# Copies of the key pages: 24 on GpSimd's queue in the index stage, 40 on SyncE's in the retention

## The chip, the cores and the metric

The kernel runs on one core of a Trainium2 chip. The metric is the time of one execution on the device, in microseconds. The kernel before took 1080.78 us, the median of three runs (1079.39 to 1082.35).

A core has engines that work side by side, each through its own list of instructions: PE (TensorE, matrix products; PEld is its loading of weights), DVE (VectorE), ACT (ScalarE), POOL (GpSimd) and SP (SyncE, which here does nothing but start DMA transfers). Sixteen DMA engines move the data that SP, ACT and POOL ask for. SBUF is the core's memory, in 128 partitions; PSUM holds the results of PE.

## The reference

One step of a decoder layer with sparse attention and retention side by side, for a new sequence of 1024 tokens ("prompt") and for 8 x 4 new tokens ("sample") that have 1024 earlier tokens each in a paged cache.

```python
def hybrid_layer(x, c, pos, attn_fn, ret_fn, w_ada, b_ada, g_norm, w_in, g_ret, w_pa, w_pr, w_out):
    B, T, _ = x.shape
    h, gate = modulated_input(x, c, w_ada, b_ada, g_norm)
    qa, ka, va, za, qi, ki, wi, qr, kr, vr, zr, ga, gr = split_projection(h @ w_in)
    heads = lambda a, n: a.reshape(B, T, n, -1)
    ka, va = heads(ka, N_HEADS_A), heads(va, N_HEADS_A)
    y_a = attn_fn(heads(qa, N_HEADS_A), ka, va, heads(qi, N_HEADS_IDX), ki, wi) * jax.nn.silu(za)
    q_r = rotary(heads(qr, N_HEADS_R), pos)
    k_r = rotary(heads(kr, N_HEADS_R), pos) * DK_R ** -0.5
    ret, ret_state = ret_fn(q_r, k_r, heads(vr, N_HEADS_R).astype(jnp.float32))
    y_r = group_norm_heads(ret).astype(x.dtype) * g_ret * jax.nn.silu(zr)
    merged = jax.nn.sigmoid(ga) * (y_a @ w_pa) + jax.nn.sigmoid(gr) * (y_r @ w_pr)
    x = x + gate[:, None, :] * (merged @ w_out)
    return x, (ka, va, ki, ret_state)

def dsa_sample(q, k_new, v_new, qi, ki_new, wi, cache_k, cache_v, cache_kidx, page_table):
    ...
    ki_past = cache_kidx[page_table].reshape(DB, PAST_LEN, HEAD_DIM_IDX)
    ki_all = jnp.concatenate([ki_past.astype(ki_new.dtype), ki_new], axis=1)
    idx, valid = select_keys(index_scores(qi, wi, ki_all), pos, topk)
    ...
    kg = jnp.where(in_past[..., None, None], cache_k[phys, slot].astype(k_new.dtype), take_rows(k_new, idx_n))
    ...
    return sparse_attend(q, kg, vg, valid).reshape(DB, T, WIDTH_A)
```

D_MODEL is 1024, there are 8 heads of 64 in attention and retention and 4 of 64 in the indexer, and everything is float32. What matters here is `cache_k`: the kernel computes the logits of the sample tokens against all 1024 past keys of each of the 8 sequences, so it needs all 8 x 8 = 64 pages that the page table names. A page is 128 tokens x 8 heads x 64, 256 KB.

## The kernel before

**Projections.** `h @ w_in` is made 128 columns at a time. Each such projection (`project_parts`, L532 to L550) runs over three pieces of 352 of the 1056 tokens and, in each, over 8 slices of the contraction with three products (`terms`, L224 to L228), since weights and activations are split into a high and a low part. SP loads 128 columns of weights, 512 KB, into `ws` (`wload`, L205); ACT takes the high part (L211), and DVE, or POOL for each third projection, the low part (`wsplit`, L212). `prefetch` (L513 to L524) is called at the head of each projection. It starts loads of later projections in the order of the list `order` (L505 to L510): the index queries, four gates (O_GA), then for each pair of retention heads K, Q, V, Z of the retention (O_KR, O_QR, O_VR, O_ZR), the attention's queries (O_QA) and two gates, and after the four pairs the attention's keys, values and the rest. Loads run about two projections ahead of their use.

**Stages.** In the profiled execution the index stage lies at about 74 to 133 us and the retention at 133 to 545 us. The index stage scores the prompt's queries in blocks b = 7 to 2, with four heads h each (L903 to L927); then it gathers the indexer's cached keys with eight indirect DMAs of POOL into `kx` (L963), two buffers in turn, and PE transposes them (L969). The retention (L620) handles two heads at a time in `pair` (L673). K and Q are rotated there: SP loads the table `rot` (L692), and once the projection is done it copies halves of the rows crosswise into `tmp` (L696 and L697, the swaps); then three full-size operations make the rotated rows (L699 to L701). These run on POOL for both rows of pair 0 and pair 1 and for K of pair 2, and on DVE for the others (`e = nc.vector if p + a > 2 else nc.gpsimd`). PE then makes state products (L735), DVE scans them (L737), ACT copies the result to `SD` (L739); PE makes the scores (L747), DVE multiplies them with the decay masks (L753), and PE forms the outputs (L763, L766). Further work of a pair is on POOL: `qm` (L781), `vm` (L785), and the two full-size steps of the group norm (L813 and L821), the last of which PE waits for in order to transpose (L829). Beside all this DVE and ACT pick the 256 best keys of each token by counting passes (L996 to L1091, with short steps such as L1022, L1062 and L1089).

**The page copies.** `KG` (L576) is a buffer in DRAM that holds each sequence's past keys with the head halves apart; SP reads it back as `kv` (L1221), from 558 us on, when the retention is over. `copy_page` (L580 to L592) fills it, one page a call. It is one call ahead of itself: ACT copies the page table's column for the next page to a small tile `ptn` (L585); for the page of the call before, POOL reads the number of the page from its tile (L589) and starts a DMA from `cache_k` to `KG`, DRAM to DRAM, 256 KB (L590). There are 12 calls in the index scoring, at every second head (L923), then one in nine of sixteen pieces of every projection (`turn`, L546 and L547), and at the end, after the first key projection of the attention, whatever is left (L1290 and L1291). In the trace the 64 issues lie between 74.5 and 541.1 us.

**Order.** Each engine executes its instructions in one fixed order. A scheduler makes it from the program as it is written and from when operands should be ready, and may move an instruction ahead of others that are written earlier; `tc.issue_after(x)` is a constraint that the instructions under it stand behind x in that order.

Of the kernel before, what the change touches and what calls it, by code (L numbers as in the profile page):

```python
# [34 lines left out]
O_QA, O_KA, O_VA, O_ZA, O_QI, O_KI, O_QR, O_KR, O_VR, O_ZR, O_GA, O_GR = (  # L35
    0, 512, 1024, 1536, 2048, 2304, 2372, 2884, 3396, 3908, 4420, 5444)
# [88 lines left out]
def _hybrid_step(ctx, tc, A, outs, dbg):  # L125
    nc = tc.nc
# [17 lines left out]
    def pj():  # L144

        turns[0] += 1
        if third[0] and turns[0] % 3 == 0:
            return third[0].tile([128, 512], F32, name="pj3", bufs=1)
        return psj.tile([128, 512], F32, name="pj", bufs=2)

    def pl():
        return ps.tile([128, 1024], F32, name="pl", bufs=2)

    def pt():
        return ps.tile([128, 512], F32, name="pt", bufs=2)
# [47 lines left out]
    def wload(pool, src, f0, n, k=KT, name="ws", bufs=2):  # L203
        ws = pool.tile([128, k, 128], F32, name=name, bufs=bufs)
        nc.sync.dma_start(ws[:, :, :n], wcols(src, k, f0, n))  # L205
        return ws

    def wsplit(pool, ws, n, k=KT):
        wh = pool.tile([128, k, 128], F32R, name="wh", bufs=2)
        wl = pool.tile([128, k, 128], F32R, name="wl", bufs=2)  # L210
        nc.scalar.copy(wh[:, :, :n], ws[:, :, :n])  # L211
        (nc.vector if k == 4 or len(order) % 3 else nc.gpsimd).tensor_sub(wl[:, :, :n], ws[:, :, :n], f32(wh[:, :, :n]))  # L212
        return wh, wl
# [10 lines left out]
    def terms(p, w, k, sl):  # L224
        wh, wl = w
        nc.tensor.matmul(p, wh[:, k], HH[k][:, sl], start=(k == 0), stop=False)  # L226
        nc.tensor.matmul(p, wh[:, k], HL[k][:, sl], start=False, stop=False)  # L227
        nc.tensor.matmul(p, wl[:, k], HH[k][:, sl], start=False, stop=(k == KT - 1))  # L228
# [16 lines left out]
    def last_on(engine):  # L245
        return next(i for i in reversed(nc.cur_bb.bb.instructions) if i.engine == engine)
# [4 lines left out]
    with ExitStack() as s0:  # L251
# [121 lines left out]
        rows_, turn = {}, [0]  # L373
# [56 lines left out]
        v, t, u = [RB[:, T + 9 * i:T + 9 * i + 9] for i in range(3)]  # L430
# [62 lines left out]
        for k in range(KT):  # L493
            for step in steps[k].split():
# [3 lines left out]
                else:  # L498
                    at, o = int(step[1]), int(step[2])
# [13 lines left out]
    def prefetch():  # L513

        while order and len(fetched) < (2 if room[0] else 1):
            f0 = order.pop(0)
            room[1] += 1
            pool = room[0] if room[0] and room[1] % 3 == 0 else wp
            with tc.issue_after(loads[-1].ins):
                fetched.append((f0, wload(pool, w_in, f0, 128, bufs=2 if pool is wp else 1)))  # L520
        if fetched:
            f0, ws = fetched.pop(0)
            with tc.issue_after(head_ends[0].ins), tc.issue_after(head_ends[1].ins):
                split.append((f0, wsplit(wp, ws, 128)))  # L524
# [7 lines left out]
    def project_parts(f0, use, chunks=chunks):  # L532

        if not split:
            prefetch()
        g0, w = split.pop(0)
        assert g0 == f0
        prefetch()
        for c, sl in enumerate(chunks):
            p = pj()[:, :sl.stop - sl.start]  # L540
            for k in range(KT):
                terms(p, w, k, sl)
            end = last_on(mybir.EngineType.PE)
            use(c, p)
            turn[0] += 1
            if turn[0] * 9 // 16 != (turn[0] - 1) * 9 // 16:  # L546
                copy_page()  # L547
            if marks is not None:
                marks.append([last_on(e) for e in (mybir.EngineType.DVE, mybir.EngineType.Activation)])
            yield end  # L550
# [24 lines left out]
    KG = dram.tile([NB, 4, 4, 256, 128], F32, name="KG")  # L575
    pages = []  # L576

    seen, turn = [], [0]

    def copy_page():  # L580
        if pages:
            at = pages.pop(0)
            t = cst.tile([NB, 1], I32, name="ptn", bufs=2)
            with tc.issue_after(last_on(mybir.EngineType.Activation)):
                nc.scalar.copy(t, pages_of[0][:, at[1]:at[1] + 1])  # L585
            seen.append((at, t))
        if len(seen) > (1 if pages else 0):
            (b, g), t = seen.pop(0)
            v = nc.gpsimd.value_load(t[b:b + 1], min_val=0, max_val=A["cache_k"].shape[1] - 1)  # L589
            nc.gpsimd.dma_start(KG[b, g // 2, :, 128 * (g % 2):128 * (g % 2) + 128],  # L590
                              A["cache_k"][0][bass.ds(v, 1)].rearrange("o t (j h) d -> (o j) t (h d)", j=4))

    pages_of = []

# [3 lines left out]
    def split_rows(pool, f0, p, dst, new, x=None):  # L598

        hl = [pool.tile([128, TT], F32R, name="raw", bufs=rows_kept[0]) for _ in "hl"]  # L600

        def use(c, y):
            sl = slice(c * CH, c * CH + CH)
            nc.scalar.copy(hl[0][:, sl], y)
            if x is not None:
                nc.scalar.copy(x[:, sl], y)
            nc.vector.tensor_sub(hl[1][:, sl], y, f32(hl[0][:, sl]))
            if c == 2:
                for k in range(4):
                    nc.scalar.copy(new[32 * p:32 * p + 32, k], y[32 * k:32 * k + 32, CH - NS:])  # L610
        yield from project_parts(f0, use)
        for places, t in zip(dst, hl):
            for d in places:
                nc.sync.dma_start(d[128 * p:128 * p + 128], f32(t[:, :T]))
# [232 lines left out]
    with ExitStack() as s1:  # L847
# [4 lines left out]
        with ExitStack() as s2:  # L852
# [37 lines left out]
            for g in range(3):  # L890
                p = pt().rearrange("p (t c) -> p t c", c=128)
                for t in range(4 * g, min(4 * g + 4, 9)):
                    n = 128 if t < 8 else NS
# [13 lines left out]
            for b in range(7, 1, -1):  # L907
                W = (b + 1) * 128
                for h in range(4):
                    m = -(-W // 512)  # L910
                    p = pl().rearrange("p (m c) -> p m c", c=512)[:, :m, :W // m]
                    q = QS[h][:, b * 128:b * 128 + 128]
                    for n in range(m):
                        sl = slice(n * W // m, (n + 1) * W // m)
                        nc.tensor.matmul(p[:, n], q, KH[:, sl], start=True, stop=False)
                        nc.tensor.matmul(p[:, n], q, KL[:, sl], start=False, stop=True)
                    rl = ip.tile([128, LK], F32, name="rl", bufs=2)
                    nc.scalar.activation(rl[:, :W].rearrange("p (m c) -> p m c", m=m), p, AF.Relu)
                    if h == 0:
                        nc.vector.tensor_scalar(SC[b], rl[:, :W], wsc[:, b, 0:1], None, op0=OP.mult)  # L920
                    else:
                        scored = nc.vector.scalar_tensor_tensor(SC[b], rl[:, :W], wsc[:, b, h:h + 1], SC[b], op0=OP.mult, op1=OP.add)
                    if h % 2:  # L923
                        copy_page()
                if b == 7:
                    whole_row = scored.ins
                nc.vector.tensor_add(SC[b][:, W - 128:W], SC[b][:, W - 128:W], C[:, C_CAUS:C_CAUS + 128])  # L927
# [23 lines left out]
            for G in (0, 1):  # L951
                p = pt()[:, :128]
                nc.tensor.matmul(p, SX[:NS, 128 * G:128 * G + 128], dw.rearrange("p h t -> p (h t)"), start=True, stop=True)
                t = ip.tile([128, 4, NS], F32, name="wt", bufs=2)
# [4 lines left out]
            for G in (0, 1):  # L959
                KP = []  # L960
                for b in range(4 * G, 4 * G + 4):
# [5 lines left out]
                    p = pt()  # L967
# [162 lines left out]
    def token_rows(tl2, x, p, out_p, out_s, dst):  # L1130
        rows = slice(128 * p, 128 * p + 128)

        def use(t0, m, n, y):
            tk = tl2.tile([128, 4, 128], F32, name="tk", bufs=2)
            nc.scalar.copy(tk[:n, :m], y[:n, :m])
            if n == 128:
                nc.sync.dma_start(out_p[0, 0, 128 * t0:128 * t0 + 512, 2 * p:2 * p + 2].rearrange("(t p) h d -> p t (h d)", p=128), tk)
            else:
                nc.sync.dma_start(out_s[0, :, :, 2 * p:2 * p + 2].rearrange("b i h d -> (b i) (h d)"), tk[:n, 0])
            if dst is not None:  # L1140
                nc.sync.dma_start(dst[128 * t0:128 * t0 + m * n, rows].rearrange("(t p) c -> p t c", p=n), tk[:n, :m])
        to_tokens(x, use)
# [141 lines left out]
    for p in range(4):  # L1284
        x = tl2.tile([128, TT], F32, name="kx", bufs=1)
        for c, _ in enumerate(split_rows(tl, O_KA + 128 * p, p, k_rows, ks, x)):
            if c < 2:
                next(past)
        token_rows(tl2, x, p, k_out, ks_out, None)
        while p == 0 and (pages or seen):  # L1290
            copy_page()  # L1291
        next(past), next(past)
    for p in range(4):
        x = tl.tile([128, TT], F32, name="raw", bufs=rows_kept[0])
# [276 lines left out]
    for n_, j in enumerate(line):  # L1571
        if j not in merged:
            load_merged(j)
        t, u = merged[j]
# [133 lines left out]
```

## Time and profile before

| | us |
|---|---|
| median of three runs | 1080.78 (1079.39 to 1082.35) |
| profiled execution, its own time | 1082.81 |
| its span in the trace | 1081.2 |
| DVE busy | 697.9 |
| ACT busy | 457.1 |
| POOL busy, of it page copies | 271.3, 73.0 |

The span is the time from the first to the last event of the trace; the execution's own time is 1.6 us longer. The mean clock granted to PE was 0.991 of full speed. Rows of the profile name an instruction by engine, line and operation, then output <- input with sizes, and `xN` for a number of them. In a timeline a row begins with its start and duration in us, and ends in brackets with how long the engine sat idle before it and whose work ended that. SPq and POOLq are the queues in which these engines issue DMAs and loads.

### The profile page before, as it was taken

The page shows a single profiled execution, that of the slowest core. Times are in us where ns is not written, and L with a number is a line of the kernel's source. Part 1 is how long each engine was busy: PE and PEld are TensorE (multiplying, and loading weights), DVE is VectorE, ACT ScalarE, POOL GpSimd, SP SyncE. Part 2 cuts the span into 40 slices and gives each one's busy share as a digit, 9 for nine tenths or more (in the row PEclk, how much of TensorE's full clock was granted, in tenths as well). Part 3 has the DMA queues.
Part 4 walks back from the last instruction along what each step waited for, and adds up shares of the span by engine and source line. Part 5 has one row for each costly group of instructions (what it writes and reads, how often), then busy time and mean ns, then how long its engine had stood idle before and what let it go on. Part 6 is the DMA issues. An engine that isn't in the chain of part 4 may idle for free. (4 is left out here: it accounts for less than half of the span.)

```text
span 1081.2 us, 20359 instructions
## 1 busy us (share of the span) xinstructions
PE 1051.9 (97%) x7903; PEld 965.6 (89%) x7903; DVE 697.9 (65%) x1538; ACT 457.1 (42%) x981; POOL 271.3 (25%) x227
## 2 busy tenths in 40 slices
PE   7999999999999999998999999999999999999997
PEld 6899799799989989998899998887999999998776
DVE  6875259668877987799834444211356766597665
ACT  5675355454555555323223322221345665442111
POOL 0015427132722531313210003244023333100000
PEclk9999999899999999998999999999999999999999
DMA  9935665375637644563379879786958520556531
GB/s 305 263 86 154 199 178 151 87 206 149 180 97 228 168 129 145 170 176 86 129 254 310 277 240 312 228 297 230 337 201 270 199 90 31 181 177 241 175 108 59
DMA packets 173620, 202.79 MB, mean 188 GB/s; under 512 B 32068, under 2 KB 140500, under 8 KB 172436
## 3 DMA queue, kind: packets, MB, share of 16 engines
q1 hardware_dynamic: 150352, 164.59, 48.0%
q0 software_dynamic: 22656, 36.05, 11.1%
q8 instruction: 62, 1.02, 0.4%
q10 hardware_dynamic: 516, 0.86, 0.2%
q14 instruction: 34, 0.28, 0.1%
HBM read 156.12 MB, written 57.95 MB: 198 GB/s over the span
## 5 line engine op out<-in xcount | busy, mean ns | idle before, releaser
L226 PE MATMUL pj<-hh,wh 128*128 128x352 f32 (+1 forms) x1168 | 384.5, 329 | 0.0
L228 PE MATMUL pj<-hh,wl 128*128 128x352 f32 (+1 forms) x1168 | 379.1, 325 | 0.2 <-POOL wl L212 0.2
L227 PE MATMUL pj<-hl,wh 128*128 128x352 f32 (+1 forms) x1168 | 379.0, 324 | 0.0
L226 PEld LDWEIGHTS pj<-hh,wh 128*128 128x128 f32 x1168 | 220.7, 189 | 10.6 <-issue 9.1
L228 PEld LDWEIGHTS pj<-hh,wl 128*128 128x128 f32 x1168 | 220.7, 189 | 6.9 <-issue 6.1
L227 PEld LDWEIGHTS pj<-hl,wh 128*128 128x128 f32 x1168 | 221.1, 189 | 3.8 <-issue 3.1
L1008 DVE TENSOR_SCALAR_CACHE_REDUCE eq<-sc,cand 128x896 bf16<-128x896 f32 (+4 forms) x155 | 135.8, 876 | 2.6
L590 POOL DMA_DIRECT2D KG<-in_cache_k x64 | 73.0, 1141 | 222.6 <-issue 134.9
L211 ACT CAST wh<-ws 128x1024 fp32r<-128x1024 f32 (+1 forms) x65 | 61.1, 941 | 128.8 <-PE pj L227 81.4
L212 POOL TENSOR_TENSOR wl<-ws,wh 128x1024 fp32r<-128x1024 f32 x18 | 43.3, 2406 | 191.4 <-ACT wh L211 150.4
L212 DVE TENSOR_TENSOR wl<-ws,wh 128x1024 fp32r<-128x1024 f32 (+1 forms) x47 | 56.0, 1191 | 44.9 <-ACT wh L211 39.7
L1393 POOL TENSOR_SCALAR lg<-lg,st 128x1024 f32<-128x1024 f32 (+7 forms) x64 | 47.2, 754 | 110.1 <-DVE st L1390 100.6
L1227 DVE STREAM_TRANSPOSE kt<-kv 128x1024 f32<-128x1024 f32 x32 | 38.6, 1232 | 43.1 <-DMA kv<-KG 42.8
L1385 ACT ACTIVATE lg<-lg,st 128x1024 f32<-128x1024 f32 (+7 forms) x64 | 49.5, 775 | 28.8 <-DVE st L1379 24.5
L1619 PE MATMUL pj<-woh,MH 128*128 128x512 f32 (+1 forms) x136 | 51.4, 378 | 0.0
L1620 PE MATMUL pj<-wol,MH 128*128 128x512 f32 (+1 forms) x136 | 51.2, 377 | 0.0
L1621 PE MATMUL pj<-woh,ML 128*128 128x512 f32 (+1 forms) x136 | 51.2, 377 | 0.0
L1197 POOL DMA_INDIRECT kv<-in_cache_v,idx x32 | 31.6, 988 | 58.8 <-PE sx L1261 41.2
L1015 ACT ACTIVATE ra<-sc,cand 128x1024 bf16<-128x1024 f32 x31 | 35.6, 1147 | 13.5 <-DVE cand L1091 13.4
L1636 ACT ACTIVATE u<-xo 128x512 f32<-128x512 f32 (+2 forms) x19 | 11.6, 609 | 66.4 <-DVE xo L1635 44.0
L839 ACT ACTIVATE raw<-pj 128x352 f32<-128x352 f32 x48 | 22.1, 461 | 35.4 <-PE pj L228 28.9
L1015 ACT ACTIVATE ra<-scs,cand 32x1056 bf16<-32x1056 f32 x31 | 36.4, 1175 | 0.8
(363 smaller groups left out, 1898.8 us busy)
## 6 DMA issues: line engine op xcount, KB each, us to landing
ws<-in_w_in SPq DMA_DIRECT2D x49, 512.0 KB
KG<-in_cache_k POOLq DMA_DIRECT2D x64, 256.0 KB
kv<-KG SPq DMA_DIRECT2D x32, 512.0 KB
rot<-in_rot SPq DMA_DIRECT2D x8, 1056.0 KB
x<-in_w_ada SPq DMA_DIRECT2D x16, 512.0 KB
TG<-raw SPq DMA_DIRECT2D x15, 528.0 KB
wst<-in_w_out SPq DMA_DIRECT2D x12, 512.0 KB
u<-TG SPq DMA_DIRECT2D x8, 528.0 KB
```

The source lines that it names most:

```text
L211: nc.scalar.copy(wh[:, :, :n], ws[:, :, :n])
L212: (nc.vector if k == 4 or len(order) % 3 else nc.gpsimd).tensor_sub(wl[:, :, :n], ws[:, :, :n], f32(wh[:, :, :n]))
L226: nc.tensor.matmul(p, wh[:, k], HH[k][:, sl], start=(k == 0), stop=False)
L227: nc.tensor.matmul(p, wh[:, k], HL[k][:, sl], start=False, stop=False)
L228: nc.tensor.matmul(p, wl[:, k], HH[k][:, sl], start=False, stop=(k == KT - 1))
L590: nc.gpsimd.dma_start(KG[b, g // 2, :, 128 * (g % 2):128 * (g % 2) + 128], A["cache_k"][0][bass.ds(v, 1)].rearrange("o t (j h) d -> (o j) ...
L1008: nc.vector.tensor_scalar(junk[:n, :W], sc, thr[:n, j:j + 1], 0.0, op0=op, op1=OP.add, accum_out=cnt[:n, j:j + 1])
L1015: nc.scalar.activation(junk[:n, :W], sc, AF.Sign, bias=thr[:n, NV + j:NV + j + 1], scale=-1.0, accum_out=cnt[:n, NV + j:NV + j + 1])
L1385: nc.scalar.activation(l, l, AF.Exp, bias=st[:, i, 1:2], scale=-1.0, accum_out=st[:, i, 3:4])
L1619: nc.tensor.matmul(x, MH[:, k, tk], wh[:, k], start=(k == 0), stop=False)
L1620: nc.tensor.matmul(x, MH[:, k, tk], wl[:, k], start=False, stop=False)
L1621: nc.tensor.matmul(x, ML[:, k, tk], wh[:, k], start=False, stop=(k == KT - 1))
```

## The change

24 calls of `copy_page` remain: one for each of the heads 1 to 3 in the index scoring (18), and six in the pieces of the first four gates. At the first projection after that, `copy_page(0)` issues the page that is one behind. The other 40 pages go through `copy_behind`: at the head of the projections of V, Z, the attention's queries and the two gates of each pair, behind the weights load that `prefetch` has just placed, SP reads the numbers of two pages straight from the page table in SBUF (`pts`) and starts the two DMAs. Source, destination and pattern of a transfer are as before (`copy_to`). No `ptn` tile is needed for those 40. The loop that copied what was left is replaced by an assertion that nothing is.

```diff
         prefetch()
+        if f0 < O_KA or O_VR <= f0 < O_GA or f0 >= O_GA + 4 * 128:
+            copy_page(0)
+            copy_behind(2)
         for c, sl in enumerate(chunks):
...
             use(c, p)
-            turn[0] += 1
-            if turn[0] * 9 // 16 != (turn[0] - 1) * 9 // 16:
+            if O_GA <= f0 < O_GA + 4 * 128 and (c + f0 // 128) % 2:
                 copy_page()
...
-    seen, turn = [], [0]
-
-    def copy_page():
-        if pages:
+    seen = []
+
+    def copy_to(e, v, b, g):
+        e.dma_start(KG[b, g // 2, :, 128 * (g % 2):128 * (g % 2) + 128],
+                    A["cache_k"][0][bass.ds(v, 1)].rearrange("o t (j h) d -> (o j) t (h d)", j=4))
+
+    def copy_behind(n):
+        with tc.issue_after(last_on(mybir.EngineType.SP)):
+            for b, g in pages[:n]:
+                copy_to(nc.sync, nc.sync.value_load(pages_of[0][b:b + 1, g:g + 1], min_val=0, max_val=A["cache_k"].shape[1] - 1), b, g)
+        del pages[:n]
+
+    def copy_page(ahead=1):
+        if ahead and pages:
             at = pages.pop(0)
             t = cst.tile([NB, 1], I32, name="ptn", bufs=2)
             with tc.issue_after(last_on(mybir.EngineType.Activation)):
                 nc.scalar.copy(t, pages_of[0][:, at[1]:at[1] + 1])
             seen.append((at, t))
-        if len(seen) > (1 if pages else 0):
+        if len(seen) > ahead:
             (b, g), t = seen.pop(0)
-            v = nc.gpsimd.value_load(t[b:b + 1], min_val=0, max_val=A["cache_k"].shape[1] - 1)
-            nc.gpsimd.dma_start(KG[b, g // 2, :, 128 * (g % 2):128 * (g % 2) + 128],
-                              A["cache_k"][0][bass.ds(v, 1)].rearrange("o t (j h) d -> (o j) t (h d)", j=4))
+            copy_to(nc.gpsimd, nc.gpsimd.value_load(t[b:b + 1], min_val=0, max_val=A["cache_k"].shape[1] - 1), b, g)
...
-                    if h % 2:
+                    if h:
                         copy_page()
...
-        while p == 0 and (pages or seen):
-            copy_page()
+        assert p or not pages and not seen
```

## The prediction

> **What bounds the kernel now.** I read the engine summary of the page first, then one answer of the windows view over the stage in which the copies are issued, then the groups, then the list of PE's waits, and last the timelines of the engines around the waits that belong to this stage.
>
> ```profile
> PE 1051.9 (97%) x7903; PEld 965.6 (89%) x7903; DVE 697.9 (65%) x1538; ACT 457.1 (42%) x981; POOL 271.3 (25%) x227
> ```
> ```profile
> 74.00:133.00 59.00, 58.71 (x371) 52.54 (x370) 28.34 (x49) 26.86 (x57) 30.30 (x26) 1.00 0.57 161
> 133.00:545.00 412.00, 398.79 (x3034) 376.11 (x3027) 333.76 (x725) 189.57 (x385) 142.91 (x94) 0.98 0.54 153
> ```
> ```profile
> L590 POOL DMA_DIRECT2D KG<-in_cache_k x64 | 73.0, 1141 | 222.6 <-issue 134.9
> ```
>
> PE (TensorE) is busy 1051.9 of 1081.2 us, so time is won only where PE now waits or runs at a lower clock. The windows row gives length, busy time of PE, PEld, DVE, ACT and POOL, granted clock, share of DMA and GB/s. In the index stage (74 to 133 us) PE idles 0.3 us; in the retention (133 to 545) it idles 412.00 - 398.79 = 13.2 us, and the clock is 0.98. All 64 copies lie in these two stages. A copy occupies POOL for 1.14 us, because POOL itself issues it: 73.0 us altogether. That is no cost to PE by itself. It costs where DVE or POOL work that PE needs stands behind a copy, and the waits of PE say where that can be:
>
> ```profile
> PE pb L747 <- DVE tmp L753: 5.6, 3, 3.3
> ...
> PE pt L829 <- POOL O L821: 2.1, 1, 2.1
> ...
> PE pt L969 <- DMA kx<-in_cache_kidx,gidx: 0.3, 1, 0.3
> ```
>
> (Sum, count, longest.) PE's scores L747 wait for the masks L753 on DVE, the last transposes L829 for the norm L821 on POOL. Now the timelines of POOL, DVE and PE in pair 0:
>
> ```profile
> 181.79 1.13 POOL L590 DMA_DIRECT2D KG<-in_cache_k  x1
> 182.94 2.46 POOL L701 TENSOR_TENSOR qrT<-qrT,tmp 128x1056 f32<-128x1056 f32 x1
> 185.35 2.41 POOL L212 TENSOR_TENSOR wl<-ws,wh 128x1024 fp32r<-128x1024 f32 x1
> ```
> ```profile
> 182.02 5.77 DVE L1089 TENSOR_TENSOR base<-base,inc 128x7 int32<-128x7 int32 x1
> ...
> 195.10 1.28 DVE L753 TENSOR_TENSOR tmp<-pb,dm 128x512 f32<-128x512 f32 x2
> ```
> ```profile
> 190.46 1.75 PE L747 MATMUL pb<-qrT,krT 64*64 64x128 f32 x40
> ...
> 195.84 1.97 PE L747 MATMUL pb<-qrT,krT 64*64 64x128 f32 x16 [1.19 <-DVE tmp L753]
> ```
> ```profile
> L1089 DVE TENSOR_TENSOR base<-base,inc x31: 155/167/5772, 157.2 to 456.4; 128x7 int32<-128x7 int32 x31
> ```
> ```profile
> 187.80:195.10 7.30, 5.79 (x96) 4.64 (x94) 7.24 (x17) 5.13 (x10) 4.80 (x5) 1.00 0.61 155
> ```
>
> L1089 adds 7 numbers in each partition; its median is 0.167 us (min/median/max in ns), yet this one lasts 5.77 us, from 182.02 to 187.79: it starts while POOL issues a copy and ends when POOL's unbroken string (copy, L701, L212) ends. So a copy between two POOL operations lengthens the time for which DVE is shut out by its own 1.13 us. Behind it DVE is full (7.24 of 7.30) up to the masks at 195.10, for which PE waits 1.19. That is the loss that this change can take away.
>
> **The change part by part.** *Copies leave POOL in the retention.* 24 of 64 stay on POOL (18 in the index scoring, 6 in the first four gates), 40 go to SP. I go through each place where a copy stands in front of work that PE is late for.
>
> ```profile
> 286.05 1.13 POOL L590 DMA_DIRECT2D KG<-in_cache_k  x1
> ```
> ```profile
> L212 DVE TENSOR_TENSOR wl<-ws,wh 128x1024 fp32r<-128x1024 f32 (+1 forms) x47 | 56.0, 1191 | 44.9 <-ACT wh L211 39.7
> ```
> ```profile
> 286.27 4.51 DVE L212 TENSOR_TENSOR wl<-ws,wh 128x1024 fp32r<-128x1024 f32 x1
> ...
> 400.02 0.74 DVE L1022 TENSOR_SCALAR inc<-cnt 128x5 int32<-128x5 f32 x1
> ```
> ```profile
> 307.74 1.83 PE L763 MATMUL pb<-qrT,SD 128*128 128x128 f32 x14 [1.15 <-ACT SD L739]
> ...
> 400.84 1.09 PE L747 MATMUL pb<-qrT,krT 64*64 64x128 f32 x16 [1.10 <-DVE tmp L753]
> ...
> 503.32 1.97 PE L747 MATMUL pb<-qrT,krT 64*64 64x128 f32 x16 [3.35 <-DVE tmp L753]
> ```
> ```profile
> 536.65 0.18 DVE L820 TENSOR_SCALAR rs_y<-rs_y 128x18 f32<-128x18 f32 x1
> ```
> ```profile
> 399.66 1.13 POOL L590 DMA_DIRECT2D KG<-in_cache_k  x1
> ...
> 493.86 1.11 POOL L590 DMA_DIRECT2D KG<-in_cache_k  x1 [0.86 <-ACT kd L713]
> ...
> 537.84 1.14 POOL L590 DMA_DIRECT2D KG<-in_cache_k  x1 [9.61 <-issue]
> 539.00 2.12 POOL L821 TENSOR_TENSOR O<-O,rs_y 128x1152 f32<-128x1152 f32 x1
> ```
> ```profile
> 541.17 1.09 PE L829 MATMUL pt<-C,O 128*128 128x128 f32 x8 [2.11 <-POOL O L821]
> ```
>
> - Pair 0: one copy, 1.13 us, and PE waits 1.19 for what stands behind it: gain 1.13.
> - Pair 1: the same string around 286.05; DVE's L212 takes 4.51 us where its group's mean is 1.191; PE waits 1.15 at 307.74 for SD, made from DVE's scan: gain 1.13.
> - Pair 2: a copy at 399.66 holds L1022 0.74 us where the equally small L1089 has a median of 0.167, at the moment when PE waits 1.10: gain 0.57.
> - Pair 3: a copy of 1.11 heads a string of POOL at 493.86, ahead of the wait of 3.35. Bounds 0 and 1.11; I take the 0.57 of pair 2.
> - End of pair 3: rs_y is there at 536.83, but POOL takes the copy first and L821 starts at 539.00. Without the copy it starts 2.17 earlier; PE waits 2.11: gain 2.11.
>
> Sum 1.13 + 1.13 + 0.57 + 0.57 + 2.11 = 5.5 us. The other removed copies, with their loads and ACT's ptn columns (40 of 64 go), stand where PE does not wait: nothing.
>
> *Index stage.* POOL gets 18 copies where it had 12, 6 x 1.2 = 7 us more, and stands at 30.3 of 59. The cover is that idle half; what it can expose is the gather of kx, which shares POOL's queue:
>
> ```profile
> 94.02 1.18 POOL L590 DMA_DIRECT2D KG<-in_cache_k  x1
> ...
> 97.24 1.53 POOL L963 DMA_INDIRECT kx<-in_cache_kidx,gidx  x1 [2.04 <-PE pt L969]
> ```
>
> Gathers and copies take turns, and PE already waits 0.3 for one kx. Two buffers limit how far gathers run ahead, so a copy more in front of a gather is 1.18 us later for PE. Bounds: 0 (POOL's idle time takes them all) and 4 x 1.18 = 4.7 (one ahead of every second of the eight gathers). I take one, +1.2. The six copies in the gates replace ones that were there; nothing.
>
> *SP.* A copy on SP is a value load and a DMA issue.
>
> ```profile
> L589 POOLq TENSOR_LOAD <-ptn x64: 287/293/1217, 72.8 to 538.7; - x64
> ```
> ```profile
> 465.27 0.39 SPq L205 DMA_DIRECT2D ws<-in_w_in  x1
> ...
> 472.89 0.52 SPq L696 DMA_DIRECT2D tmp<-qrT  x1
> ...
> 474.72 0.77 SPq L697 DMA_DIRECT2D tmp<-qrT  x1
> ```
>
> The load was 0.29 us on POOL, SP's issues here last 0.39 to 0.77, so a copy is about 1 us of SP: 40 us in the 412 of the stage, on a queue that does nothing but issue. That time is covered; uncovered, two copies would put 2 us in front of a swap. What is queued behind a waiting SP instruction are the swaps of the rotation (L696, L697), the state loads and the next weights. The weights run two projections ahead. The swaps do not, and this is what the copies' traffic can reach:
>
> ```profile
> 482.95 1.26 DVE L699 TENSOR_TENSOR qrT<-qrT,rot 128x1056 f32<-128x1056 f32 x1 [0.73 <-DMA tmp<-qrT]
> ```
> ```profile
> 252.00:254.00 2.00, 2.00 (x15) 2.00 (x14) 1.93 (x5) 0.00 (x0) 1.11 (x1) 1.00 0.97 278
> 254.00:258.00 4.00, 4.00 (x27) 4.00 (x26) 2.79 (x11) 3.00 (x6) 0.00 (x0) 1.00 0.24 67
> ```
>
> From 252 to 254 a weights load fills the 16 DMA engines (0.97, 278 GB/s); from 254 to 258 only one copy moves, at a share of 0.24, four engines, 67 GB/s. 256 KB at that rate is 3.8 us, two copies on the same four engines about 7.6. A pair behind the load of 465.27 (1.9 us) leaves those engines some time after 474.5, while the swaps enter from 472.9 to 475.5; DVE already waits 0.73 for them. Bounds for the late swaps: 0 (copies gone in time, or on other engines), and 2.5 in each of pairs 1 to 3. I take 1.5, nearest to pair 3 alone, where DVE has no slack.
>
> Here a rule of the Trainium skill speaks against the change. Its page "DMA: Bandwidth & Descriptors", in the section "Why a DMA increments its semaphore by 16 and not by 1", says that a transfer uses the largest number of engines up to 16 that divides the slowest dimension of both sides (4 here), and that SP's queue always takes the lowest-numbered ones, where GpSimd's takes consecutive engines in turn. The share of 0.24 agrees with four; no run here shows which. By that rule every copy on SP lands on the same four engines as the one before it; by the 0.24 alone they might spread, and the 1.5 would be 0.
>
> **Sum.** -5.5 + 1.2 + 1.5 = -2.8 us. The profiled execution took 1082.81 us (span 1081.2 and 1.6 around it), so 1080.0 by it; it lies 2.0 above the median of the runs (1080.78), so the forecast is **1078.0**, range of its own 1075.0 to 1080.0.
>
> **The rivals.** *B, the clock comes back too.* After the long waits of pairs 0 and 3 the granted clock is 0.50:
>
> ```profile
> 195.50:202.30 6.80, 6.46 (x31) 6.13 (x32) 3.50 (x8) 2.28 (x2) 0.00 (x0) 0.50 0.31 86
> ...
> 502.70:509.50 6.80, 6.18 (x31) 5.85 (x32) 6.73 (x10) 2.27 (x2) 0.00 (x0) 0.50 0.35 104
> ```
>
> 6.46 and 6.18 us of PE work there would be 3.2 and 3.1 at full clock. If shorter waits keep the clock up in one of the two, the time is 1078.0 - 3.1 = 1074.9, in both 1071.7. For it: both stretches follow directly on waits that shrink. Against it: pair 3 keeps 2.8 of its 3.35, and pairs 1 and 2 kept their clock with waits of 1.1.
> The Trainium skill, "TensorE: Matmul & The Clock Gate", part 1 on the HAM clock gate, gives half clock after an idle window of about 3.4 us, with windows that run freely. Two stretches of 6.8 us, twice that window, agree, though no wait here is quite that long.
>
> *C, the next wait takes the place.* DVE in pairs 0 to 3 is full before the masks (7.24 of 7.30 above), and the string of POOL holds it with or without the copy; the scheduler may fill the 1.13 us with other DVE work. Then only the end of pair 3 is won: -2.11 + 1.2 = -0.9, 1079.9. The same comes out if the change does not do what it says, POOL's copies staying in front of rotations because the first four gates push theirs late.
>
> *D, slower: the swaps wait behind the copies.* If a pair of copies enters the four engines just ahead of the q swaps in every pair, these land up to 7.6 us late. Pairs 2 and 3 rotate on DVE, which is full up to the masks: about 7 us each for PE. In pairs 0 and 1 POOL rotates, qrT is complete at 185.40 and PE's scores needed it at 190.46, five us of slack: 2 each. 18 - 5.5 + 1.2 = +13.7: 1094.5. It decides from where the losses pass 5.5 - 1.2 = 4.3, 2.2 in each of pairs 2 and 3, that is, where the copies enter less than 5.4 us ahead of the swaps. For it: the load of 465.27 is 7.6 us ahead, not much more. Against it: that is still outside.
>
> **How the numbers follow.** Forecast 0.45; B 0.20; C 0.20; D 0.12; mishaps that I have not seen, 0.03, counted as slower. A measurement of this kernel tells 0.3% from no change, which is 1077.5 to 1084.0. The forecast lies at that edge: I give 0.23 of its chance to faster, 0.22 to same. Faster: 0.23 + 0.20 = 0.43. Same: 0.22 + 0.20 = 0.42. Slower: 0.12 + 0.03 = 0.15. The range goes from 1070 (both stretches of B and some of the costs at 0) to 1085 (index and swaps at their upper bounds: -5.5 + 4.7 + 7.5 = +6.7 would be 1087, of which I leave the last out as part of D).
>
> **What would show it.** Right: no POOL copy after about 145 us; L1089 in pair 0 about 1.1 us shorter; L821 of pair 3 directly after rs_y and no wait of PE at L829; the waits at L747 in pairs 0, 2, 3 shorter by 1.1, 0.6, 0.6. Index stage: PE's waits for kx at L969 at about 1.5. Swaps: DVE's L699 of pair 3 waiting about 2 instead of 0.73; D shows there as 7. B shows in the clock rows. Wrong would be a new wait of PE for weights (L205 held behind a copy's load), which I priced at nothing.

## The result: 1068.4 us, and the profile after

| | before | after |
|---|---|---|
| median, four runs each | 1081.57 us | 1068.39 us (1066.64 to 1069.95) |
| ratio, 95% interval | | 0.9879 (0.9853 to 0.9904) |
| span of the profiled execution | 1081.2 us | 1065.0 us |
| mean granted clock | 0.991 | 0.998 |

The change makes the kernel 13 us faster. The time lies 1.6 us below the lower end of the range of 1070 to 1085, and the gain is more than four times the 2.8 us that I forecast. First the engine summary of the page after, then a windows row over its retention (length; busy PE, PEld, DVE, ACT, POOL; clock; DMA share; GB/s) and its list of PE's waits (sum, count, longest).

```profile
PE 1045.2 (98%) x7903; PEld 960.4 (90%) x7903; DVE 690.1 (65%) x1538; ACT 455.0 (43%) x941; POOL 227.0 (21%) x187
```
```profile
134.00:529.00 395.00, 391.75 (x3029) 370.99 (x3029) 325.43 (x725) 186.40 (x339) 91.11 (x48) 1.00 0.53 155
```
```profile
PE pb L757 <- DVE tmp L763: 1.8, 2, 1.2
...
PE pt L979 <- DMA kx<-in_cache_kidx,gidx: 1.1, 2, 0.6
PE pt L745 <- ACT kd L723: 0.8, 1, 0.8
PE pt L839 <- POOL O L831: 0.6, 1, 0.6
```

The lines of the retention are ten higher after the change: L757 is the old L747 (scores), L763 the masks, L839 the last transposes. The retention went from 412.0 to 395.0 us. Its idle time on PE fell from 412.00 - 398.79 = 13.2 to 395.00 - 391.75 = 3.25 us: 10.0 less waiting. The busy time fell from 398.79 to 391.75 for the same products: 7.0 less, because the clock of the row is 1.00 and no longer 0.98. The two stretches at half clock are gone. The index stage lost 0.8 us to two waits for kx. Together -10.0 - 7.0 + 0.8 = -16.2, which is the difference of the two spans (the profiled execution after is the fastest of its four, the medians differ by 13.2).

### The profile page after: what moved, and what is told of

It reads as the page before. It is cut to its first block, busy times and chain, and to the rows that moved or that the text cites. A ratio compares the mean times of both kernels' runs of the same rounds, so it can differ in the third digit from the quotient of the medians.

```text
span 1065.0 us, 20301 instructions
## 1 busy us (share of the span) xinstructions
PE 1045.2 (98%) x7903; PEld 960.4 (90%) x7903; DVE 690.1 (65%) x1538; ACT 455.0 (43%) x941; POOL 227.0 (21%) x187
## 2 busy tenths in 40 slices
DMA packets 183381, 202.55 MB, mean 190 GB/s; under 512 B 23909, under 2 KB 152821, under 8 KB 182197
## 5 line engine op out<-in xcount | busy, mean ns | idle before, releaser
L212 DVE TENSOR_TENSOR wl<-ws,wh 128x1024 fp32r<-128x1024 f32 (+1 forms) x47 | 52.7, 1122 | 41.6 <-ACT wh L211 41.4
L1237 DVE STREAM_TRANSPOSE kt<-kv 128x1024 f32<-128x1024 f32 x32 | 38.6, 1233 | 45.3 <-DMA kv<-KG 45.0
L1388 DVE CUSTOM_DVE_ANT_0 lg<-x,bi 128x512 f32<-128x512 f32 (+3 forms) x64 | 35.3, 570 | 1.5 <-PE x L1387 1.1
```

## Experiments

Each run is timed against the kernel before on the same chip; the ratio has its 95% interval. "The small DMA" below is POOL's copy of 8 KB to a scratch buffer, whose issue takes POOL 0.56 to 0.63 us. The expectations set two theories against each other: P, that the cost of a copy was POOL's time, and T, that it was the copy's traffic on the DMA engines.

**Leave the 40 copies out.** Are the copies on SP free?

```diff
-        with tc.issue_after(last_on(mybir.EngineType.SP)):
-            for b, g in pages[:n]:
-                copy_to(nc.sync, ...)
         del pages[:n]
...
-nc.sync.dma_start(kk, KG[4 * G + b4, u]...)
+nc.sync.dma_start(kk, KG[4 * G + b4, u]... if 4 * G + u < 3 else A["cache_k"][0][i:i + 2]...)
```

> The changed kernel without the 40 copies on SP; the reads of those pages take other rows of the cache, so the logits of 40 of 64 pages are not computed from the right keys. Theory P (POOL's time was the cost: its 1.13 us copies hold DVE and POOL's own chain): copies on SP are nearly free, so 1066.5 to 1068.5, against 1068.4 of the changed kernel; the wait of DVE for the q swaps of pair 3 falls from 2.13 to about 0.7. Theory T (their traffic was the cost, in front of the weights and swaps): 250 KB times 40 less to move gives more, under 1065.

1064.4 us, 0.9845 (0.9829 to 0.9862). That is what T said, and below P's 1066.5: against the changed kernel (0.9879) 0.34%, some 4 us, are still to be won. The two intervals just overlap; the four times of each do not (1063.6 to 1065.3 against 1066.6 to 1070.0). The changed reads of the cache have no part in it: from PE's last transposes of the retention to the end it takes 540.0 us here and 539.8 in the changed kernel. So the copies on SP still cost after the change, by their traffic or by their issues.

**The same places, issued by POOL.**

```diff
-copy_to(nc.sync, nc.sync.value_load(
+copy_to(nc.gpsimd, nc.gpsimd.value_load(
```

> The changed kernel with the 40 copies issued by POOL at the same places of the program, two behind each of the 20 projections' heads. Theory P: back to the time of before, 1077 to 1083, with the granted clock at half again somewhere in the retention. Theory S (what helped is the new places and the order that the scheduler makes of them): 1067 to 1071.

1108.3 us, 1.0246 (1.0223 to 1.0269). As a test it failed: without ACT's tile that paced them, the scheduler put POOL's copies ahead of everything, all 40 between 147 and 226 us, and PE stood 39.4 us, while the rotation of K in pair 0 stood behind most of them in that queue (its last step starts at 214.30). It only shows that the copies need a pace.

**POOL's occupation without traffic, first attempt.** 44 DMAs of POOL with runs of 4 bytes.

> The changed kernel, copies on SP as they are, and 44 additional DMAs of POOL in the retention at every ninth of sixteen pieces, as before, each with 512 runs of 4 bytes, so nearly no traffic. Theory P: POOL is occupied as before, 1077 to 1083, and waits of PE at the scores and the last transposes as before. Theory T: hardly any traffic, 1067 to 1070.

1266.8 us, 1.1711 (1.1652 to 1.177). Failed too: they depend on nothing, so they were issued at the very start, and for some 220 us their runs of 4 bytes filled the DMA engines (share 0.9 and more at 29 to 79 GB/s). It says nothing on P.

**The pattern of SP's copies turned.** Source, destination and bytes stay; only the order of the dimensions changes.

```diff
+        if e is nc.sync:
+            e.dma_start(KG[b, g // 2, :, ...].rearrange("j t c -> t j c"),
+                        A["cache_k"][0][bass.ds(v, 1)].rearrange("o t (j h) d -> (o t) j (h d)", j=4))
+            return
```

> The changed kernel with the patterns of SP's copies turned so that the 128 tokens are the outer dimension. If the four engines are what the q swaps wait behind, the wait of DVE at L709 and its like in pair 3 goes from 2.13 to under 1.2, and the time falls by 0.5 to 1.0 (1067.4 to 1067.9); if not, both stay. A copy alone would then move at a DMA share clearly over 0.24.

1064.9 us, 0.9851 (0.9833 to 0.9869): as good as leaving the copies out, and a larger gain than expected. The timelines of DVE show the rotation of Q in pair 3, in the changed kernel and in this one:

```profile
471.57 1.26 DVE L709 TENSOR_TENSOR qrT<-qrT,rot 128x1056 f32<-128x1056 f32 x1 [2.13 <-DMA tmp<-qrT]
```
```profile
467.06 1.23 DVE L713 TENSOR_TENSOR qrT<-qrT,rot 128x1056 f32<-128x1056 f32 x1
```

The wait for the swaps, 2.13 us, is gone. That was my first sign that the place where a copy runs on the DMA engines weighs more than the engine that issues it.

**POOL's occupation, paced.** The small DMA behind a load of a number that waits for ACT's tile, one call ahead, as `copy_page` did; 44 of them in the retention.

```diff
+            if f0 < O_KA or O_QR <= f0 < O_GA or f0 >= O_GA + 4 * 128:
+                turn[0] += 1
+                if few[0] < 44 and turn[0] * 9 // 16 != (turn[0] - 1) * 9 // 16:
+                    ghost()
```

> The changed kernel, copies on SP as they are, plus up to 44 small DMAs of POOL in the retention, paced as the copies of before were (a column of the page table copied by ACT, POOL's load of a number, one call ahead, nine in sixteen pieces), each moving 8 KB instead of 256. Theory P (POOL's occupation): POOL is taken for about 1 us each time, so most of the loss is back, 1076 to 1083. Theory T (traffic): under 1070. Half way would mean both.

1074.0 us, 0.9926 (0.9905 to 0.9948): between the two. Of the 5.6 us against the changed kernel, one wait of PE makes 3.4, and a stretch at half clock behind it some 1.7. POOL, DVE, ACT and PE at that place:

```profile
273.28 0.58 POOL L594 DMA_DIRECT2D KX<-in_cache_k  x1 [4.42 <-ACT tmp L720]
273.88 2.46 POOL L734 TENSOR_TENSOR qrT<-qrT,rot 128x1056 f32<-128x1056 f32 x1
276.30 2.46 POOL L735 TENSOR_TENSOR tmp<-tmp,rot 128x1056 f32<-128x1056 f32 x1
278.84 2.44 POOL L736 TENSOR_TENSOR qrT<-qrT,tmp 128x1056 f32<-128x1056 f32 x1
```
```profile
273.85 4.95 DVE L1124 TENSOR_TENSOR base<-base,inc 128x7 int32<-128x7 int32 x1
```
```profile
279.09 1.15 ACT L1050 ACTIVATE ra<-sc,cand 128x1024 bf16<-128x1024 f32 x1 [6.79 <-DVE cand L1126]
```
```profile
282.97 0.44 PE L704 MATMUL pt<-C,tmp 128*128 128x128 f32 x2 [3.43 <-ACT tmp L720]
```

A step of 7 numbers is held 4.95 us while POOL works off its string, ACT waits 6.79 for the step after it, its copy of the V projection comes late, and PE waits 3.43; a half-clock stretch of 3.4 us follows. So the holding is real and can reach PE. Whether it does seems to hang on which DVE step meets the string; no run varied that alone.

**Copies on SP at the places of before.** One page at nine of sixteen pieces, not two behind the weights.

```diff
-            copy_page(0)
-            copy_behind(2)
+            copy_page(0)
...
+                if turn[0] * 9 // 16 != (turn[0] - 1) * 9 // 16:
+                    copy_behind(1)
```

> The changed kernel with the 40 copies on SP one by one at the nine in sixteen pieces of the retention, where POOL had them before, instead of two behind the weights of each projection. Traffic and places are those of before, only the queue differs. Theory P: 1066 to 1071. Theory T or S: 1076 or more.

1121.2 us, 1.0362 (1.0344 to 1.0379), some 40 us slower than before although POOL is free of these copies. So taking them off POOL is not enough. What a copy costs on POOL's queue this run does not say. SP's timeline:

```profile
243.05 11.62 SPq L588 DMA_DIRECT2D KG<-in_cache_k  x5
254.77 2.81 SPq L855 DMA_DIRECT2D TG<-raw  x1
257.79 7.30 SPq L588 DMA_DIRECT2D KG<-in_cache_k  x3
265.20 2.82 SPq L205 DMA_DIRECT2D ws<-in_w_in  x1
```

ACT, where it waits for weights:

```profile
272.63 1.04 ACT L211 CAST wh<-ws 128x1024 fp32r<-128x1024 f32 x1 [12.27 <-DMA ws<-in_w_in]
```

The places are those of before in the program, but in SP's order the copies come in bunches, and one takes SP 2.3 us with its load: five last 11.62 us. SP stands, and the weights and swaps behind them come out late; ACT waits 12.27 us, and PE 9.0 at 288.7 and 10.1 at 401.4. This is rival D of the prediction, in SP's queue itself rather than behind it.

**The same, with the pattern turned.** The two lines of the turned pattern replace the old ones in `copy_to`, on top of this run, so here the 24 copies on POOL are turned as well.

> The 40 copies on SP one by one at the pieces of the retention, as in the run of 1121.2, but with the 128 tokens as outer dimension. If four engines that are full hold SP's issues there (a median of 1.57 us and up to 3.43 for one) and with them the weights, this falls to 1063 to 1070 and an issue to about 0.6; if the places in SP's order are what delays the weights, it stays over 1100.

1064.0 us, 0.9839 (0.979 to 0.9888), from 1121.2. The issues of the two runs, by minimum, median and maximum in ns:

```profile
L588 SPq DMA_DIRECT2D KG<-in_cache_k x40: 637/1566/3432, 109.6 to 502.2; - x40
```
```profile
L588 SPq DMA_DIRECT2D KG<-in_cache_k x40: 536/553/3007, 107.8 to 451.4; - x40
```

With the tokens outside, these places cost nothing any more (1064.9 was the time with two behind the weights). How much of the 57 us the turned copies on POOL have is not told apart; they lie ahead of 145 us, where PE waits 0.9 us for kx in the run of 1121.2.

**All 64 copies on SP, pattern turned**, three behind the weights of a projection, none on POOL. This is the version that the runs pointed to.

```diff
+        if pages_of and pages and (f0 < O_KA or O_VR <= f0):
+            copy_behind(3)
```

> All 64 copies on SP, three behind the weights of each projection from the first gate on (not K and Q of the retention), with the 128 tokens as outer dimension; none on POOL, no tiles for them on ACT. Against the 1064.9 with that pattern and 24 on POOL: the wait for kx (0.6) and the index stage's loss of 0.8 go, so 1063.5 to 1064.5, if copies near the kx gathers cost them nothing; over 1065.5 if three in a row delay weights or swaps.

1063.0 us (1062.89 to 1063.64), 0.9825 (0.9809 to 0.9842): the lowest median of all, and 0.5 below what was expected; the waits for kx are gone. Its interval lies clear of the changed kernel's, not of the two runs above with the turned pattern and 24 copies on POOL.

**Two small DMAs in the string of pair 0.**

```diff
+            for _ in range(2 if (p, a) == (0, 1) else 0):
+                with tc.issue_after(last.ins):
+                    last = small()
```

> The changed kernel with two small DMAs of POOL (8 KB each) between the second and the third step of the rotation of Q in pair 0, 2.2 us of POOL in the string there, and nothing else. Theory P: PE waits 1 to 2.3 more in pair 0, as in the kernel before. If such waits are also what halves the granted clock there, 3.2 more: 1072 to 1074.5; if not, 1069 to 1071. Theory T: 1068.4.

1070.3 us (1068.1 to 1075.6), 0.9906 (0.9871 to 0.994). The string is 1.20 us longer and PE waits only 0.40 in pair 0, without half clock. The trace is that of an execution of 1068.5, which also has a wait for kx of 1.68 at 99 us that has nothing to do with the string. In the two longer executions (1072.0 and 1075.6) the mean granted clock was 0.995 and 0.992 instead of 0.998, and no trace shows where it fell. The median lies in P's range without half clock (1069 to 1071), the traced execution at T's 1068.4 and with less of a wait than P's 1 to 2.3. This run does not decide between them.

**Two small DMAs in a row at every place**, as long as one old copy.

```diff
             small(v)
+            small(v)
```

> As the run with small DMAs of POOL (0.58 us each, 1074.0), but two in a row at each place, 1.16 us, which is what one copy took before. Theory P (POOL's time alone): 1077 to 1084, about as long as the kernel before, with a stretch of half clock after each wait of PE of 2 us and more. If the rest of the loss was the copies' traffic from POOL's queue: 1073 to 1076.

1068.5 us, 0.9873 (0.9826 to 0.9921), the time of the changed kernel: 88 issues of some 0.56 us, 44 times the 1.13 us of a copy, cost nothing measurable in all. P said 1077 to 1084. PE's waits moved, though: 0.30 at the masks of pair 0 and 0.72 for SD in pair 1 are back, two of the places that the prediction had priced, while those of pair 2 fell from 1.96 to 0.22.

**The kernel before with nothing but the pattern turned.** All 64 copies on POOL, at their old places.

> The kernel before, all 64 copies on POOL at their old places, with the 128 tokens as outer dimension, and nothing else changed. Theory P (POOL's time): the same occupation, so 1077 to 1083. Theory T (what cost was the traffic of a copy that piles up on a quarter of the DMA engines in front of swaps and weights): the swaps of K in pair 0 land within 3 us of their last issue and not 5, and most of the gain comes without SP: 1066 to 1071.

1066.3 us, 0.985 (0.9817 to 0.9883): one statement turned in the kernel before gives what the whole change gave, and POOL still has the copies. SP's last swap of K in pair 0 and POOL's first step of its rotation:

```profile
155.90 0.59 SPq L697 DMA_DIRECT2D tmp<-krT  x1
```
```profile
159.07 2.48 POOL L699 TENSOR_TENSOR krT<-krT,rot 128x1056 f32<-128x1056 f32 x1
```

They lie 3.17 us apart, and POOL does not wait for the swaps here; in the kernel before they lie 5.00 apart, with a wait for them (shown further down). A copy that moves alone here (issued at 199.45) reaches a DMA share of 0.71, 221 GB/s, and is gone within 2 us, where the prediction's took 4 us at 0.24. All PE's waits of pairs 0, 1 and 3 at the scores and outputs are gone; pair 2 keeps 0.87 and 1.08, with half clock behind them in this profiled execution, the longest of the four. A reservation: the turned copy also takes POOL less time, as the groups of the two pages (count | busy, mean ns | idle) show, before and here:

```profile
L590 POOL DMA_DIRECT2D KG<-in_cache_k x64 | 73.0, 1141 | 222.6 <-issue 134.9
```
```profile
L590 POOL DMA_DIRECT2D KG<-in_cache_k x64 | 48.9, 764 | 222.9 <-issue 110.0
```

**So the same with a small DMA behind each copy.**

```diff
+            nc.gpsimd.dma_start(KX[8 * b + g], ...[:, :4])
```

> The kernel before with the 128 tokens as outer dimension (1066.3, where POOL needs 0.76 us for a copy instead of 1.14), and behind each copy one more small DMA of POOL (8 KB, 0.58 us), so that POOL is taken for 1.3 us a copy, longer than before. Theory T (pile-up of traffic): 1066 to 1071. If the shorter occupation of POOL was what helped there: 1077 or more.

1066.6 us, 0.9845 (0.9814 to 0.9876). The groups of copies and small DMAs:

```profile
L591 POOL DMA_DIRECT2D KG<-in_cache_k x64 | 49.2, 769 | 196.0 <-issue 104.4 <-ACT ra L1017 32.0 <-ACT rl L920 23.4
L593 POOL DMA_DIRECT2D KX<-in_cache_k x64 | 38.6, 603 | 0.2 <-PE pt L831 0.2
```

POOL is taken for 49.2 + 38.6 = 87.8 us, 15 more than before, and the time stays. The shorter issue was not what helped. One part of the loss does come back, in pair 0, where the DVE step of 5.77 us before is as long again, and PE waits for the masks behind it:

```profile
180.68 5.99 DVE L1091 TENSOR_TENSOR base<-base,inc 128x7 int32<-128x7 int32 x1
```
```profile
194.73 1.09 PE L749 MATMUL pb<-qrT,krT 64*64 64x128 f32 x16 [1.06 <-DVE tmp L755]
```

Before, that wait was 1.19 and half clock came behind it; here the clock stays up.

## Why the prediction was wrong, point by point

**What bounds the kernel: right.** The whole gain of the traces comes from PE's waits in the retention and from the half clock there (the index stage went the other way).

**The mechanism of the gain: wrong for most of it.** The step that failed is "That is the loss that this change can take away", said of the copy's 1.13 us in POOL's string. I took the copy that stands in the string for the whole reason that DVE was late, priced each place with it, and put the traffic of the copies on POOL at nothing. What the runs show in its place: most of the loss came from that traffic, which was in front of the swaps and the weights. With the pattern turned the copies on POOL cost 16 us less (1066.3), also with POOL taken for longer than before (1066.6), and POOL taken for as long by small DMAs leaves the time of the changed kernel (1068.5). POOL's occupation is worth something at single places: with it, PE waits 1.06 at the masks of pair 0 (1066.6), or 0.30 there and 0.72 in pair 1 (1068.5). So the price of about 1 us for a copy in the string was of the right size where it shows, but it makes a small part of the 13 us.

The lateness of the swaps was in the trace of before, 20 us ahead of the row that I quoted. SP's last swap of K in pair 0 and POOL's first step of the rotation, before:

```profile
157.16 0.59 SPq L697 DMA_DIRECT2D tmp<-krT  x1
```
```profile
162.16 2.47 POOL L699 TENSOR_TENSOR krT<-krT,rot 128x1056 f32<-128x1056 f32 x1 [1.52 <-DMA tmp<-krT]
```

and after the change:

```profile
157.26 0.59 SPq L707 DMA_DIRECT2D tmp<-krT  x1
```
```profile
159.91 2.46 POOL L709 TENSOR_TENSOR krT<-krT,rot 128x1056 f32<-128x1056 f32 x1 [12.28 <-DMA tmp<-krT]
```

The swaps take 162.16 - 157.16 = 5.00 us to the start of the rotation before, and 2.65 after. What lay ahead of them on the DMA engines, before (POOL) and after (SP):

```profile
151.50 1.14 POOL L590 DMA_DIRECT2D KG<-in_cache_k  x1 [6.80 <-issue]
152.90 1.11 POOL L590 DMA_DIRECT2D KG<-in_cache_k  x1 [0.25 <-issue]
```
```profile
147.62 3.44 SPq L583 DMA_DIRECT2D KG<-in_cache_k  x2
```

The two copies of before were issued 2 to 3 us ahead of the first swap (154.6), those of after 4 to 8 us ahead of theirs (155.3), and had more time to finish behind the weights. The same holds for the weights at a pair's end. ACT's split, in the kernel before and in the changed one, with SP's issue of the load ahead of each:

```profile
231.38 0.38 SPq L205 DMA_DIRECT2D ws<-in_w_in  x1
```
```profile
239.03 1.05 ACT L211 CAST wh<-ws 128x1024 fp32r<-128x1024 f32 x1 [6.83 <-DMA ws<-in_w_in]
```
```profile
226.65 0.38 SPq L205 DMA_DIRECT2D ws<-in_w_in  x1
```
```profile
232.07 1.05 ACT L211 CAST wh<-ws 128x1024 fp32r<-128x1024 f32 x1 [4.61 <-DMA ws<-in_w_in]
```

7.65 us from issue to split before, 5.42 after, and 6.01 in the kernel before with the pattern turned. ACT works in order, so its part of the selection came late, DVE waited for that, and PE for DVE:

```profile
241.60 0.15 DVE L1024 TENSOR_SCALAR inc<-cnt 128x1 int32<-128x1 f32 x1 [5.51 <-ACT ra L1015]
```
```profile
244.48 0.24 PE L829 MATMUL pt<-C,O 32*128 32x32 f32 x1 [0.97 <-DVE tmp L832]
```

I had priced nothing at the pairs' ends but L821 of pair 3. There the forecast's own mechanism holds: after the change this step (now L831) starts at 522.99, 0.14 us after rs_y is there, and PE's wait falls from 2.11 to 0.64.

**The rule of the Trainium skill that I weighed** ("DMA: Bandwidth & Descriptors", section on the semaphore's 16) was the right one on the wrong side. I set it against the change, for the copies' future on SP, and gave it 1.5 us; it applied to the copies on POOL as well; the copy that I had measured at 0.24 was one of POOL's. What it says, that the slowest dimension sets the number of engines, agrees with the turned pattern: on SP 1068.4 became 1064.9 and 1121.2 became 1064.0 (with the 24 on POOL turned too), on POOL 1082.1 became 1066.3, and the share of a copy alone rose from 0.24 to 0.71. That SP's four are always the same ones is not shown by any run.

**The terms**, forecast and measured, from the waits of the two traces:

| place | forecast | measured | |
|---|---|---|---|
| pair 0 | -1.13 | -2.3 | the waits for kd (0.30, 0.77) and masks (1.19) all go |
| pair 1 | -1.13 | -1.15 | |
| pair 2 | -0.57 | -0.3 | 0.78 and 1.18 stay |
| pair 3, masks | -0.57 | -2.8 | 3.35 becomes 0.59 |
| end of pair 3 | -2.11 | -1.5 | 0.64 stays |
| ends of pairs 0 and 2 | 0 | -2.1 | two waits of 0.97 and 1.12, not priced |
| index stage | +1.2 | +0.8 | |
| late swaps | +1.5 | in the rows of pairs 2 and 3 | |
| clock | 0 | -7.0 | rival B |

The table's largest error is the clock. Among the waits it is pair 3. DVE's picking of keys and the pairs' work share one queue, so what DVE loses to a late weights load at the end of pair 2 can still be there at the masks of pair 3. DVE's split of those weights, before and after:

```profile
441.98 1.23 DVE L212 TENSOR_TENSOR wl<-ws,wh 128x1024 fp32r<-128x1024 f32 x1 [5.17 <-PE pt L829]
```
```profile
430.77 1.23 DVE L212 TENSOR_TENSOR wl<-ws,wh 128x1024 fp32r<-128x1024 f32 x1 [1.89 <-ACT wh L211]
```

It starts 11.2 us earlier, at a point where PE was some 8 us ahead, and DVE keeps that lead: its rotation of Q in pair 3 starts 11.4 us earlier (482.95 and 471.57). (The name behind 5.17 is that of the last event; ACT's split before it waited 6.61 for the load.) I cut the gain to the copy nearest to the wait. That pair 1 came out at -1.15 for -1.13 proves nothing for its term: the turned pattern takes this wait away too, with the copies still on POOL. The index stage was priced about right, with the right wait. In pair 2 DVE already waited 2.23 for the swaps of Q before (380.28), which I had not looked at, and 3.71 after; that fits the small gain there. "About 2 instead of 0.73" for the swaps of pair 3 came out as 2.13, and the turned pattern shows what these waits cost: with it, pairs 2 and 3 wait 0.15 us in all, against 2.55 in the changed kernel.

**Rival B, with 0.20, was the case that came, in both pairs.** Its price of 6.3 us was right within a us. What I held against it, that pair 3 would keep 2.8 us of its wait, followed from the same wrong term. The clock alone does not make the difference: in the traces the waits, the index stage included, gave 9.2 us where the forecast had 2.8.

**Rival C** did not come: only pair 2 kept waits of the old size.

**Rival D** was wrong for this kernel and right as a mechanism: by their places alone, the same 40 copies on SP take 1068 or 1121 us.

**What stays open.** How the gain divides between swaps, weights and POOL's string was not tried one by one. On POOL the turned pattern also does without 192 small packets a copy (the page before counts 32,068 packets under 512 bytes, that run 19,780), so there the spread over the engines and the fewer packets are not told apart; on SP, where the number of packets hardly changes (183,381 and 183,860), it is the spread, with SP's shorter issue that comes with it. And the two paced runs with small DMAs (1074.0 and 1068.5) show that the string of POOL can still cost 5 us, and that one small DMA at each place can cost more than two, which I can't predict.

## What to carry to other kernels

Where a consumer waits for a DMA, measure from its issue to the consumer's start and look for what else is on the DMA engines, before taking the busy engine beside it for the cause. In this kernel a transfer that moved at a quarter of the engines' share held up what came behind it; try such a pattern with a long outer dimension first, which is one statement. And price a chain by all of its stages: DVE carried its lateness here from the end of one pair to the masks of the next, and the clock's loss, 7.0 us of the gain, went with the waits.

## What the runs showed of the hardware that I had not expected

**The clock fell after windows in which PE was not idle.** The half-clock stretches last 3.41 us or a multiple of it. Laid on that grid, the windows view of the kernel before gives, for the window ahead of the first half-clock stretch, one in pair 2 that had none behind it, and the one ahead of the second:

```profile
192.10:195.51 3.41, 1.79 (x37) 1.31 (x34) 3.41 (x10) 1.51 (x5) 0.51 (x1) 1.00 0.46 132
396.89:400.30 3.41, 1.98 (x40) 1.37 (x36) 3.37 (x8) 1.80 (x6) 2.94 (x2) 1.00 0.00 0
499.29:502.70 3.41, 0.68 (x24) 0.54 (x20) 3.38 (x6) 0.00 (x0) 0.95 (x1) 1.00 0.26 63
```

PE was busy 1.79 and 0.68 of 3.41 us where the clock fell, 1.98 where it did not. In the run with POOL's copies at the new places this window was followed by half clock:

```profile
234.60:238.01 3.41, 1.96 (x46) 1.57 (x44) 3.41 (x9) 1.55 (x5) 0.00 (x0) 1.00 0.14 37
```

In the kernel before with the pattern turned, half clock followed in pair 2 on waits of 0.87 and 1.08, behind a window with 1.46 busy; so waits of about 1 us can cost the clock too; the prediction took from pairs 1 and 2 that they don't. So if the busy time decides, the edge lies near 1.96 to 1.98, and the busy time alone may not settle it. In the Trainium skill, "TensorE: Matmul & The Clock Gate", part 1, the half rate follows an idle window; here it followed a window in which PE was half busy, and the measurement decides.

**An issue on SP is not of constant length.** In the two runs with single copies its median was 0.55 us with the pattern turned and 1.57 without, and SP does nothing else meanwhile.

**The pattern changes what the issue costs POOL**: 0.76 us instead of 1.14 for the same 256 KB.
